# Five ScalarE weight casts of the third head pair get order edges in a decoder-trunk kernel

## The chip, the core and the metric

The kernel runs on one core of one Trainium2 chip. A core has TensorE (PE; matrix products, with weight loads shown as PEld), VectorE (DVE), ScalarE (ACT), GpSimd (POOL) and SyncE (SP, which issues most of the loads). The engines run side by side, each through its own list of instructions in order, and wait for one another at semaphores. The metric is the device time of one execution in microseconds (us), as a median over several runs; less is better.

## What is computed

The reference is a decoder trunk of two layers on 256 tokens of width 1024, in float32. Layer 0 mixes tokens with three dilated window attentions, layer 1 with a gated linear attention, and each is followed by a gated feed-forward block with a short convolution. What matters here is layer 0's token mixer:

```python
def dilated_mixture(h, w_in, w_out, rel_bias):
    B, S, _ = h.shape
    qkv = (h @ w_in).reshape(B, S, A_GROUPS, 3, A_HEADS, A_HEAD_DIM)
    scale = A_HEAD_DIM ** -0.5
    outs, lses = [], []
    for g, (window, dilation) in enumerate(A_CONFIGS):
        o, lse = dilated_branch(qkv[:, :, g, 0] * scale, qkv[:, :, g, 1], qkv[:, :, g, 2],
                                rel_bias[:, g * A_HEADS:(g + 1) * A_HEADS], window, dilation)
        ...
    wts = jax.nn.softmax(jnp.stack(lses), axis=0)
    o = jnp.sum(wts[..., None] * jnp.stack(outs), axis=0)
    return o.reshape(B, S, A_WIDTH).astype(h.dtype) @ w_out
```

There are three groups (dilations 1, 4, 16) and 16 heads of width 64, taken as eight pairs. Each pair needs queries, keys and values of all three groups.

## The kernel before

**Numbers in two parts.** Each float32 weight is split in a high part, a cast to TensorE's fp32r format, and a low part, the difference. `split` (L165) does that for one block: SyncE loads `raw` (L169), ScalarE casts it to `whi` in two pieces (L176), and VectorE subtracts to get `wlo` in two pieces (L182). The activations `h` have the same two parts, and each product is three products on TensorE (`mm3`, L200 to L205): high by high, and high by low both ways. `raw` rotates over four buffers, `whi` and `wlo` over three each.

**The pairs.** The loop at L666 runs over the pairs `u` = 0 to 7. Pairs 0 and 1 are projected together from one big block `w0` (L686 to L698). From the third pair (`u` = 2) on, a pair has three projections `g` = 0, 1, 2 (L705 on), each a block of 2048 columns (pieces of 1024) that gives the queries and keys of one group, and then its values in two halves (L751 on), each a block of 1536 columns (pieces of 768). TensorE goes through the eight row tiles `kt` of a projection in order; the first half of the values serves `kt` 0 to 3, the second 4 to 7, and each piece two of them.

**Evacuation.** `evacuate` (L610) takes a projection out of PSUM. For `g` = 0, ScalarE scales the queries (L621) and casts the keys (L622, the high part), VectorE makes the low parts (L625, L627), and GpSimd copies the keys to where the scores read them (L630). For the other groups ScalarE scales the queries and VectorE copies the keys (both L615). The list `evacuated` holds the last two instructions of this, ScalarE's first.

**Softmax and turning.** `scores` (L484) makes a pair's scores on TensorE (L496 to L510); VectorE adds the bias and takes the maximum (L529), and negates it (L547); ScalarE takes the exponentials (L550, recorded in the list `exps`, four for each pair); VectorE normalises (L539 to L543). `turn_all` (L570) transposes the probabilities on TensorE (L578) and copies them out of PSUM (L582, on ScalarE and VectorE). `outputs` (L584) multiplies with the values. The scores of the first pair run behind the values of the second pair. The scores of the second pair and both turns run between the projections of the third pair, so this pair's round holds more work than the later ones.

**Filling work.** The modulation terms of later blocks are dot products of weight rows with the condition, on VectorE (L142), each followed by a small ScalarE instruction (L150 or L152). `next_half` (L465) places them between the rest.

**The order of work.** The build orders each engine's instructions by a simulated timeline, with the order of the source as priority among what is ready. `behind(...)` (L275) adds edges by hand: each instruction that is made inside it and runs on the engine of a named instruction is ordered behind that one. An edge to a ScalarE instruction holds ScalarE's instructions alone, and it adds order, no semaphore. `split` takes such edges for its two casts in `after`, and for its subtractions in `low` and `late`. In the third pair, projection 2 has edges for its subtractions only (L706). Half 0 of the values has none for its casts, and its subtractions stand behind the last dot product so far. Of half 1 the first cast stands behind the scaled query copy of projection 2 (`second`, L745), and its subtractions behind the key copy; the second cast has no edge.

Of the kernel before, what the change touches and what calls it, by code (L numbers as in the profile page):

```python
# [59 lines left out]
def trunk(ctx: ExitStack, tc: tile.TileContext, I, out):  # L60
# [104 lines left out]
    def split(src, n, dmas=1, after=((), ()), late=(), low=(), lows=True, view=None):  # L165
        raw = wraw.tile([P, 2048], F32, tag="raw", name="raw")
        for i in range(dmas):
            c = slice(n * i // dmas, n * (i + 1) // dmas)
            last_load[0] = nc.sync.dma_start(raw[:, c], src[:, c])  # L169
        hi = wspl.tile([P, 2048], F32R, tag="whi", name="whi")  # L170
        lo = wspl.tile([P, 2048], F32R, tag="wlo", name="wlo")
        part = view or (lambda w: w)
        for i in range(0, n, n // 2):
            c = slice(i, i + n // 2)
            with behind(*after[i > 0]):
                copied[0] = nc.scalar.copy(part(hi[:, c]), part(raw[:, c]))  # L176
        if not lows:
            return hi, lo, raw, n // 2
        for i in range(0, n, n // 2):
            c = slice(i, i + n // 2)  # L180
            with behind(*(late if i else low)):
                last_lo[0] = nc.vector.tensor_tensor(part(lo[:, c]), part(raw[:, c]), part(hi[:, c].bitcast(F32)), op=ALU.subtract)  # L182
        return hi, lo
# [482 lines left out]
    for u in range(NPAIR):  # L666
        if u == 0:
            with tc.issue_after(last_load[0].ins):
                bias = load_bias(0)
        place = u % 2 if u < 4 else 1  # L670
        if u == 0:
            k_hi, k_lo = ([att.tile([P, T + 4 * (i or j)], F32R, tag=f"k0{i}{j}", name="k", bufs=1) for j in range(2)] for i in range(2))
            for z in k_lo:
                nc.gpsimd.memset(z[:, T:].bitcast(F32), 0.0)
        q, k = [q_pair[place][0]], [(q_pair[place][1], k_lo[place], k_hi[place])]
        for g in (1, 2):
            q.append(att.tile([P, T], F32, tag=f"q{g}", name="q"))
            k.append(att.tile([P, T], F32, tag=f"k{g}", name="k"))
        v = [att.tile([P, NG * P], F32, tag=f"v{t}", name="v") for t in range(2)]
        if u == 0:  # L680
            b0 = [bank("pqk", tg) for tg in "ssspp"]
            pqk = [b[:, T * i : T * i + T] for b in b0[:3] for i in range(2)]
            pv = b0[3:]
            b1 = [bank("pqk", "t") for _ in range(3)]
            pqk1 = [b[:, T * i : T * i + T] for b in b1 for i in range(2)]
            for kt in range(KT):  # L686
                s, e = kt == 0, kt == KT - 1

                for a, b in ((0, 0), (1, 0), (0, 1)):
                    for i in range(2 * NG):  # L690
                        w = parts(w0[kt], P * i)
                        mm(pqk[i], w[a], h[kt][b], start=s and i % 2 == 0 and (a, b) == (0, 0), stop=e and i % 2 == 1 and b == 1)  # L692
                wv = parts(w0[kt], 6 * P, NG * P)
                for a, b in ((0, 0), (1, 0), (0, 1)):
                    for t in range(2):
                        mm(pv[t][:, : NG * P], h[kt][a][:, P * t : P * t + P], wv[b], start=s and (a, b) == (0, 0), stop=e and b == 1)
                for i in range(2 * NG):
                    mm3(pqk1[i], parts(w0[kt], 9 * P + P * i), h[kt], s and i % 2 == 0, e and i % 2 == 1)  # L698
        if u == 0:
            first_values = [by_group(v[n], pv[n], n, True) for n in range(2)]  # L700
        if u < 2:
            for g in range(NG):
                evacuate(q, k, g, (pqk, pqk1)[u][2 * g], (pqk, pqk1)[u][2 * g + 1], *first_values[1:])
        else:
            for g in range(NG):  # L705
                low = negated[-1:] if (u, g) == (2, 2) else ()  # L706
                w = split(I["wqk"][u - 2, g], 2048, low=low, late=low)
                if (u, g) == (2, 2):
                    with behind(last_lo[0]):
                        for _ in range(4):  # L710
                            second_pair[2]()
                    for _ in range(2):
                        next_half(norms[-1], turned[1])
                if (u, g) == (2, 1):
                    with tc.issue_after(last_load[0].ins):
                        bias = load_bias(1)
                    with behind(last_lo[0]):
                        for _ in range(4):
                            before[2]()
                    with behind(done):  # L720
                        second_pair = scores(1, *held, bias, *mm_k)
                pqk = bank("pqk", "p")
                pq, pk = pqk[:, :T], pqk[:, T:]
                for kt in range(KT):
                    s, e = kt == 0, kt == KT - 1


                    hk = level if (u, g) > (3, 1) and g != 1 and kt == 0 else h[kt]
                    with behind(*(last_t if (g, kt) == (2, 0) else last_s if u == 2 and kt == 0 else [])):
                        mm3(pq[:, :T], parts(w, 2 * P * kt), hk, s, False)  # L730
                    mm_k = [mm3(pk[:, :T], parts(w, 2 * P * kt + P), hk, False, e)]
                if g == 1:
                    turn_all(before, pt := new_pt(), *mm_k)
                if (u, g) == (NPAIR - 1, 2):
                    copy_level((o_hi[OLEVEL], o_lo[OLEVEL]), *turned[-2:-1])
                done = evacuate(q, k, g, pq, pk)
                if (u, g) == (2, 2):
                    turn_all(second_pair, second_pt := new_pt(), *mm_k)
                if (u, g) == (2, 0):
                    first_loads.append(last_load[0])  # L740
                if u > 2:
                    for _ in range((3, 0, 3)[g]):
                        next_half(done)
                if g == 2 - (u > 2):
                    second = list(evacuated)  # L745
            if u == 4:
                with behind(last_load[0]):
                    nc.sync.dma_start(x_all, I["xT"])
        if u > 0:
            pv = [bank("pv", "p") for _ in range(2)]  # L750
            for half in range(2):  # L751
                with behind(*chain[7]):


                    if half == 1 and u < 4:
                        hi, lo = (first_values[:1], ()) if u == 1 else (second[:1], second[1:])
                    elif u == 2:
                        hi, lo = (), last_dot[:1]
                    else:
                        hi = lo = ()  # L760
                    w = split(I["wv"][u - 1, half], 1536, after=(hi, hi if u == 1 else ()), low=lo, late=lo if u == 2 else ())
                    if u == 2 and half == 1:
                        for _ in range(4):
                            next_half(last_lo[0])
                if u > 1 and half == 0:
                    with tc.issue_after(last_load[0].ins):
                        bias = load_bias(u)
                for k4 in range(4):
                    kt = 4 * half + k4
                    wv = parts(w, 384 * k4, 384)  # L770
                    for t in range(2):
                        ht = [y[:, P * t : P * t + P] for y in h[kt]]
                        with behind(*(last_t if u == 2 and kt == 0 else [])):
                            last_pv[:] = [mm3(pv[t][:, :384], ht, wv, kt == 0, kt == KT - 1)]
        for n in range(2 if u else 0):
            by_group(v[n], pv[n], n)
        if u == 0:
            first_pair = q, k, v, bias
            continue
        if u == 1:  # L780
            held = q, k, v
            before = scores(0, *first_pair, *last_pv)
            continue
        now = scores(u, q, k, v, bias, *last_pv)
        outputs(0 if u == 2 else u - 1, before, pt, last_s[0])
        if u == 2:
            outputs(1, second_pair, second_pt, last_po[0])
            copy_level(h[0], last_cast[0])
        before = now
# [386 lines left out]
    with behind(*chain[3]):  # L1176
        w = columns(0, 1)
# [309 lines left out]
```

## Time and profile before

| | us |
|---|---|
| runs: median of 3 (lowest to highest) | 761.14 (760.03 to 762.98) |
| profiled execution, own time | 759.74 |
| its span in the trace | 758.0 |

The span goes from the first to the last instruction of the trace; the profiled execution took 1.74 us more than that. The mean granted clock of TensorE in it was 0.999 of full speed.

How to read the rows that follow. On the page, busy time and its share of the span stand for each engine, and then the chain of work that ended last, followed back from the end, by engine. A row of the windows gives a stretch, its length, then busy time and number of instructions for each engine, the clock, the busy share of the DMA engines and what they moved in GB/s. A row of waits says who waited for whom: us in total, times, longest. A row of the timeline gives the start, the time that the row takes, engine, line, operation, the tiles (out<-in), shape and number of instructions merged; in brackets stands how long the engine had been idle before and what ended that. Products on TensorE overlap, so their pace is read from the distances of their starts, not from the time of one.

### The profile page before, as it was taken

Reading aid. Unit: us, or ns where it says so; the run is one execution under the profiler, and the core shown is the slowest. Engines: PE = TensorE matmul, PEld = TensorE weight load, DVE = VectorE, ACT = ScalarE, POOL = GpSimd, SP = SyncE. Lnnn points to the kernel's source line nnn. Section 1 sums busy time; section 2 is a strip of 40 time slices with the busy share of each in tenths; the row PEclk is TensorE's granted clock in tenths of the full one; section 3 lists DMA queues with packets and bytes.
Section 4 is the critical chain, followed back from the end, with each engine's and each line's share of the span. In section 5 each row is a group of like instructions: output and inputs, shape, how many; then the busy total and the mean of one; then the engine's idle time right before and its main releaser. Section 6 shows DMA issues by size and latency. Waiting matters only on the chain.

```text
span 758.0 us, 16066 instructions
## 1 busy us (share of the span) xinstructions
PE 750.3 (99%) x6416; PEld 733.0 (97%) x6416; DVE 649.5 (86%) x1190; ACT 483.0 (64%) x945; POOL 32.7 (4%) x57
## 2 busy tenths in 40 slices
PE   8999999999999999999999999999999999999997
PEld 5999999999999999999999999999999999999996
DVE  6988999988989779999999778977869999988592
ACT  6458666565656478676767556835967767676551
POOL 0002001101101010000000000000010000000100
PEclk9999999999999999999999999999999999999999
DMA  9989599888887358877646986864646767667621
GB/s 346 403 298 328 207 338 372 269 278 296 289 285 261 112 181 294 308 271 251 220 140 234 353 295 218 327 241 163 227 168 231 276 233 268 125 146 266 204 102 56
DMA packets 39481, 187.20 MB, mean 247 GB/s; under 512 B 9020, under 2 KB 11708, under 8 KB 25838
## 3 DMA queue, kind: packets, MB, share of 16 engines
q1 hardware_dynamic: 39024, 185.73, 70.3%
q8 instruction: 50, 0.82, 0.4%
q10 hardware_dynamic: 382, 0.45, 0.2%
q14 instruction: 25, 0.20, 0.1%
HBM read 185.06 MB, written 1.10 MB: 246 GB/s over the span
## 4 chain that ended last, share of the span: by engine, by line
PE 99%; DVE 0%; ACT 0%; DMA 0%; issue 0%; DVEq 0%; ACTq 0%
PE pab L204 10%; PE pab L203 10%; PE pab L205 10%; PE pqk L203 6%; PE pqk L205 6%; PE pqk L204 6%; PE pd L204 5%; PE pd L203 5%; PE pd L205 5%; PE pv L204 4%; PE pv L203 4%; PE pv L205 4%; PE pqk L692 2%; PE py L203 2%; PE py L205 2%; PE py L204 2%
## 5 line engine op out<-in xcount | busy, mean ns | idle before, releaser
L176 ACT CAST whi<-raw 128x1024 fp32r<-128x1024 f32 (+4 forms) x264 | 237.8, 946 | 97.1 <-PE pab L204 43.4
L182 DVE TENSOR_TENSOR wlo<-raw,whi 128x1024 fp32r<-128x1024 f32 (+5 forms) x248 | 263.7, 1092 | 30.0 <-ACT whi L176 29.4
L205 PE MATMUL pab<-hhi,wlo 128*128 128x256 f32 x680 | 187.0, 276 | 0.0
L204 PE MATMUL pab<-hlo,whi 128*128 128x256 f32 x680 | 186.9, 276 | 0.0
L203 PE MATMUL pab<-hhi,whi 128*128 128x256 f32 x680 | 185.1, 277 | 0.0
L204 PEld LDWEIGHTS pab<-hlo,whi 128*128 128x128 f32 x680 | 127.5, 188 | 0.2
L205 PEld LDWEIGHTS pab<-hhi,wlo 128*128 128x128 f32 x680 | 127.7, 188 | 0.0
L203 PEld LDWEIGHTS pab<-hhi,whi 128*128 128x128 f32 x680 | 126.5, 188 | 0.1
L142 DVE CUSTOM_DVE_ANT_0 ada_raw<-ada_raw,c_bc 128x1024 f32<-128x1024 f32 x96 | 114.5, 1229 | 5.6 <-DMA ada_raw<-in_w_ada 5.6
L203 PE MATMUL pqk<-hhi,whi 128*128 128x256 f32 x374 | 102.6, 279 | 0.0
L204 PE MATMUL pqk<-hlo,whi 128*128 128x256 f32 x374 | 102.0, 278 | 0.0
L205 PE MATMUL pqk<-hhi,wlo 128*128 128x256 f32 x374 | 101.5, 278 | 0.0
L204 PE MATMUL pd<-glo,whi 128*128 128x256 f32 x308 | 84.9, 276 | 0.0
L205 PE MATMUL pd<-ghi,wlo 128*128 128x256 f32 x308 | 84.9, 276 | 0.0
L203 PE MATMUL pd<-ghi,whi 128*128 128x256 f32 x308 | 84.7, 276 | 0.0
L203 PEld LDWEIGHTS pqk<-hhi,whi 128*128 128x128 f32 x374 | 69.9, 188 | 0.2
L204 PEld LDWEIGHTS pqk<-hlo,whi 128*128 128x128 f32 x374 | 69.9, 188 | 0.0
L205 PEld LDWEIGHTS pqk<-hhi,wlo 128*128 128x128 f32 x374 | 69.2, 188 | 0.7 <-issue 0.7
L204 PEld LDWEIGHTS pd<-glo,whi 128*128 128x128 f32 x308 | 57.8, 188 | 0.0
L205 PEld LDWEIGHTS pd<-ghi,wlo 128*128 128x128 f32 x308 | 57.8, 188 | 0.0
L203 PEld LDWEIGHTS pd<-ghi,whi 128*128 128x128 f32 x308 | 57.7, 188 | 0.0
L1003 ACT ACTIVATE r<-pab,small 128x256 f32<-128x256 f32 x86 | 47.2, 559 | 10.0 <-DVE r L1006 9.6
(277 smaller groups left out, 1461.1 us busy)
## 6 DMA issues: line engine op xcount, KB each, us to landing
raw<-in_w_up SPq DMA_DIRECT2D x42, 1024.0 KB, 4.9
ada_raw<-in_w_ada SPq DMA_DIRECT2D x29, 1024.0 KB, 6.0
raw<-in_w_down SPq DMA_DIRECT2D x28, 704.0 KB, 5.4
ada_raw<-in_w_ada SPq DMA_DIRECT2D x38, 512.0 KB, 6.8
raw<-in_wqk SPq DMA_DIRECT2D x18, 1024.0 KB, 5.7
raw<-in_wv SPq DMA_DIRECT2D x14, 768.0 KB, 6.7
raw<-in_w SPq DMA_DIRECT2D x7, 960.0 KB, 6.5
raw<-in_w_v_b SPq DMA_DIRECT2D x6, 768.0 KB, 6.1
```

The lines of the kernel that those rows point to most:

```text
L142: i = nc.vector.tensor_tensor_reduce(w, w, c_bc, op0=ALU.mult, op1=ALU.add, scale=1.0, scalar=0.0, accum_out=dot,)
L176: copied[0] = nc.scalar.copy(part(hi[:, c]), part(raw[:, c]))
L182: last_lo[0] = nc.vector.tensor_tensor(part(lo[:, c]), part(raw[:, c]), part(hi[:, c].bitcast(F32)), op=ALU.subtract)
L203: mm(ps, a[0], b[0], start=start, stop=False)
L204: mm(ps, a[0], b[1], start=False, stop=False)
L205: return mm(ps, a[1], b[0], start=False, stop=stop)
L692: mm(pqk[i], w[a], h[kt][b], start=s and i % 2 == 0 and (a, b) == (0, 0), stop=e and i % 2 == 1 and b == 1)
L1003: nc.scalar.activation(r, u[:, :T], AF.Identity, scale=cw[2], bias=col(C_CB + 44 * l + f))
```

## The change

Three edits. The list `ready` takes the ScalarE instruction of the third pair's first evacuation (the cast of the keys, L622), and both casts of projection 2's weights are ordered behind it. Both casts of half 0 of the third pair's values are ordered behind the eighth exponential (`exps[7]`, the last one of the second pair). The second cast of half 1 gets the edge that the first one has, behind the scaled copy of projection 2's queries. Nothing changes for other pairs, as the second pair's two casts had their edges before, and from the fourth pair on the second piece has none.

```diff
-                w = split(I["wqk"][u - 2, g], 2048, low=low, late=low)
+                w = split(I["wqk"][u - 2, g], 2048, after=(ready, ready) if (u, g) == (2, 2) else ((), ()), low=low, late=low)
...
+                if g == 0:
+                    ready = evacuated[:1]
...
                     if half == 1 and u < 4:
                         hi, lo = (first_values[:1], ()) if u == 1 else (second[:1], second[1:])
                     elif u == 2:
-                        hi, lo = (), last_dot[:1]
+                        hi, lo = exps[7:8], last_dot[:1]
                     else:
                         hi = lo = ()
-                    w = split(I["wv"][u - 1, half], 1536, after=(hi, hi if u == 1 else ()), low=lo, late=lo if u == 2 else ())
+                    w = split(I["wv"][u - 1, half], 1536, after=(hi, hi if u < 3 else ()), low=lo, late=lo if u == 2 else ())
```

## The prediction, made before the changed kernel was run

> **What bounds the kernel now.** I read the page first (busy time, then the chain that ended last), then the windows by stage around the moved casts, then who TensorE's weight load waited for, and last the timelines of ScalarE, VectorE and TensorE from 69 to 116 us.
>
> ```profile
> span 758.0 us, 16066 instructions
> PE 750.3 (99%) x6416; PEld 733.0 (97%) x6416; DVE 649.5 (86%) x1190; ACT 483.0 (64%) x945; POOL 32.7 (4%) x57
> PE 99%; DVE 0%; ACT 0%; DMA 0%; issue 0%; DVEq 0%; ACTq 0%
> ```
>
> The chain is TensorE for 99% of the span, and all other engines share the rest. ScalarE, the only engine that the change touches, is busy for 64%. So moving ScalarE's work pays only where TensorE waits for it, and costs only where TensorE is made to wait.
>
> ```profile
> core 0: us, PE busy (x) PEld busy (x) DVE busy (x) ACT busy (x) POOL busy (x), PEclk, DMA share, GB/s
> 75.50:84.40 8.90, 8.90 (x105) 8.56 (x103) 7.51 (x23) 5.32 (x15) 1.59 (x4) 1.00 0.49 189
> 84.40:91.10 6.70, 6.70 (x62) 6.70 (x60) 6.52 (x18) 3.58 (x10) 0.00 (x0) 1.00 0.55 140
> 91.10:99.80 8.70, 8.70 (x52) 8.44 (x51) 8.70 (x14) 5.80 (x10) 0.00 (x0) 1.00 1.00 393
> ```
>
> These are the stages of projections 1 and 2 and of the values of the third pair. TensorE counts as busy all the time in each, at full clock (1.00), and VectorE is full too in the third. Busy time hides short stalls because the ends are modelled, so I look at one wait and at the starts of the products around it.
>
> ```profile
> PEld pv L204 <- DVE wlo L182: 0.3, 1, 0.3
> 91.15 0.42 PE L203 MATMUL pv<-whi,hhi 128*128 128x384 f32 x1
> 95.39 0.34 PE L205 MATMUL pv<-whi,hlo 128*128 128x384 f32 x1
> 95.56 0.34 PE L203 MATMUL pv<-whi,hhi 128*128 128x384 f32 x1
> 95.85 0.45 PE L204 MATMUL pv<-wlo,hhi 128*128 128x384 f32 x1
> 96.13 0.34 PE L205 MATMUL pv<-whi,hlo 128*128 128x384 f32 x1
> ```
>
> Products of this size start 0.17 us apart (95.39 to 95.56). The two next steps take 0.29 and 0.28: 0.12 and 0.11 us too much. This stall of 0.23 us, at the first use of the second half of the third pair's value weights, is all that the touched stages can give back by having weights earlier.
>
> **The change part by part.** Five casts move on ScalarE: two of 1024 columns (projection 2), two of 768 (values, half 0), and the second of 768 of half 1; the first one of half 1 had its edge already. Nothing is added or taken away, no cast issues a transfer, and the buffers of the loads come free behind VectorE's subtraction (L182), which comes after the cast in any case.
>
> ```profile
> 69.50 2.00 ACT L176 CAST whi<-raw 128x1024 fp32r<-128x1024 f32 x2 [0.17 <-DMA raw<-in_wqk]
> 73.28 0.62 ACT L550 ACTIVATE prob<-prob,m 128x384 f32<-128x384 f32 x1 [1.22 <-DVE m L547]
> 75.89 1.57 ACT L176 CAST whi<-raw 128x768 fp32r<-128x768 f32 x2
> 77.49 0.77 ACT L621 ACTIVATE q<-pqk 64x256 fp32r<-64x256 f32 x2
> 78.28 0.37 ACT L622 CAST k<-pqk 128x256 fp32r<-128x256 f32 x1
> 82.07 0.62 ACT L550 ACTIVATE prob<-prob,m 128x384 f32<-128x384 f32 x1 [3.41 <-DVE m L547]
> 84.39 0.19 ACT L550 ACTIVATION_READ_ACCUMULATOR prob<-prob,m 128x1 f32 x1
> 84.48 0.82 ACT L176 CAST whi<-raw 128x768 fp32r<-128x768 f32 x1
> 90.15 0.37 ACT L615 ACTIVATE q<-pqk 128x256 f32<-128x256 f32 x1
> 90.41 2.72 ACT L176 CAST whi<-raw 128x768 fp32r<-128x768 f32 x3
> 78.69 0.86 DVE L625 SCALAR_TENSOR_TENSOR q<-pqk,q 64x256 fp32r<-64x256 f32 x2 [1.33 <-ACT k L622]
> 82.00 2.35 DVE L182 TENSOR_TENSOR wlo<-raw,whi 128x1024 fp32r<-128x1024 f32 x2
> ```
>
> *Projection 2's casts, 2.00 us at 69.50, go behind L622.* Their old place empties, but the first pair's exponentials at 73.28 had waited 1.22 us for VectorE after a gap, so they come no earlier: 0. The new place is the hole of 3.41 us between L622 and the second pair's exponentials, which 2.00 fits with 1.41 to spare. They then end near 78.65 + 2.00 = 80.65. Their cover is that TensorE first wants these weights at 84.38 (row below), and VectorE's subtraction of them stands at 82.00. So 0; if the hole were closed the casts would come behind the exponentials, which is the second rival.
>
> *The values' half 0, 1.57 us at 75.89, goes behind the second pair's last exponential.* It stood ahead of L621 without a pause, so L621 and L622 come up to 1.6 us earlier, and GpSimd's copies of the keys behind L622 with them. VectorE waited 1.33 us for L622 ahead of L625; with that gone, the second pair's scores on VectorE, the exponentials (80.74 for 82.07) and their successors come about 1.3 us earlier. None of it ends in a wait of TensorE: 0. The casts then run from 84.57 at the latest to 86.14. Their users:
>
> ```profile
> 90.16 1.82 DVE L182 TENSOR_TENSOR wlo<-raw,whi 128x768 fp32r<-128x768 f32 x2
> 91.89 0.42 DVE L615 COPY k<-pqk 128x256 f32<-128x256 f32 x1
> 92.23 0.95 DVE L182 TENSOR_TENSOR wlo<-raw,whi 128x768 fp32r<-128x768 f32 x1
> 93.10 1.22 DVE L142 CUSTOM_DVE_ANT_0 ada_raw<-ada_raw,c_bc 128x1024 f32<-128x1024 f32 x1
> 94.24 0.69 DVE L582 COPY pt<-t 128x512 f32<-128x512 f32 x1
> 94.84 0.95 DVE L182 TENSOR_TENSOR wlo<-raw,whi 128x768 fp32r<-128x768 f32 x1
> ```
>
> VectorE subtracts half 0 at 90.16 and TensorE starts on it at 91.15, so 4.0 us are left: 0. Queued behind these two casts are the scaled copy of projection 1's queries (L615) and two copies of transposes (L582), which would come up to 1.6 us later, or not later at all where the exponentials come earlier.
>
> *The values' half 1.* The second cast (84.48) goes behind the queries' copy at 90.15, as the first already does, inside the run of three at 90.41 (2.72 us is more than 3 x 0.82, so the other two of that run are wider ones, the next pair's). This is where the order of use matters. VectorE's subtraction at 92.23 can only be the second piece's, as that was cast at 84.48, while the first piece's stands at 94.84, ends at 95.79, and TensorE goes on at 95.85: the first piece, wanted first, is subtracted last, behind a dot product (1.22) and a copy (0.69). With both casts behind the query copy, the first ends at about 91.2 and the second at about 92.0. If VectorE's places stay and the first piece takes the one at 92.23, it is done at 93.2, over 2 us ahead of its use, and the second piece, at 94.84, is done at 95.8. That one is wanted 12 products after 95.56 (two matrices of 128 rows by two row halves by three), 12 x 0.173 = 2.1 us later. The stall goes: -0.23.
>
> No row shows the changed order of VectorE, so I bound it: -0.23 from above, as nothing else is waiting; +1.2 from below, where one more dot product (1.22) gets ahead of the first piece. I take -0.2, as the nearest rows are those of the present places, and keep both ends.
>
> Sum: 0 + 0 + 0 - 0.2. The profiled execution took 759.74 us, 1.74 around its span of 758.0, and gets 759.5. The median of the runs is 761.14, 1.40 above that execution, so the forecast is 760.9.
>
> **The rivals.**
>
> *The change doesn't do what it says.* The edges hold ScalarE only. VectorE may still subtract the second piece first, as its order is its own. TensorE then waits as before: 761.1. For it: in the rows above the first piece was cast by 91.2 and still stood behind three other instructions. Against it: the reason for the second piece's early place, an early cast, is gone.
>
> *Projection 2's casts fall behind the second pair's exponentials.* Against it is the hole of 3.41 us, in which nothing else is ready; for it, that the exponentials stand earlier in the source. The first cast would then run 84.57 to 85.5, its subtraction (half of 2.35) would end at 86.7, and TensorE, which wants it two products after its start, would stand from about 84.6:
>
> ```profile
> 83.15 1.47 PE L578 MATMUL t<-ident,pn 128*128 128x128 f32 x12
> 84.38 0.37 PE L203 MATMUL pqk<-hhi,whi 128*128 128x256 f32 x1
> 89.92 1.47 PE L578 MATMUL t<-ident,pn 128*128 128x128 f32 x12
> 77.39 0.39 PE L203 MATMUL pqk<-hhi,whi 128*128 128x256 f32 x1
> ```
>
> That costs 2.1 us: 763.2. Only with the two value casts ahead as well (1.57), and the query copy and a transpose copy behind them (about 1), does it reach 4.7 us and 765.8. From 3.8 us it decides the sign beyond 0.5%. The Trainium skill (TensorE: Matmul & The Clock Gate, HAM oscillation) says that TensorE idle for over some 3.4 us falls back to half clock; by that, the longer form would cost an estimated 1.7 us more, and the shorter nothing. The granted clock is 1.00 in every window above, so the rows here can't show it.
>
> *Later rounds are ordered worse (slower).* The build orders each engine by a simulated timeline, so new ends of ScalarE's work at 75 to 92 us may change which of VectorE's ready instructions goes first later on. Room in a later round:
>
> ```profile
> 104.20:133.50 29.30, 29.30 (x272) 28.55 (x268) 26.79 (x55) 19.34 (x45) 3.08 (x4) 1.00 0.93 341
> 113.09 0.28 DVE L543 TENSOR_SCALAR pn<-prob,m 128x128 f32<-128x128 f32 x1
> 115.23 1.47 PE L578 MATMUL t<-ident,pn 128*128 128x128 f32 x12
> ```
>
> VectorE is busy 26.8 of 29.3 us, and the probabilities are ready 1.9 us (113.37 to 115.23) ahead of their transposes. It decides once more than 1.9 us, two dot products of 1.22, goes ahead of them: then each round loses at least 0.5, and a third dot product makes it 1.8. Five rounds of about 1.2 cost 6 us: 767. Against it: TensorE paces each stage, and the moved work is all within the third pair's.
>
> *Faster than forecast.* Projection 1's 48 products take 5.76 us (77.39 to 83.15), projection 2's 48 take 5.54 (84.38 to 89.92), 4.6 ns less for each. If projections 0 and 1 got the later pace, 0.44 would be gained: 760.5. Nothing in the change reaches TensorE's pace.
>
> **How the numbers follow.** I call 0.5% (3.8 us) what a measurement of this kernel can tell from no change. The forecast gets 0.60, the first rival 0.12, the second 0.12 (0.07 in its short form, 0.05 in the long one), the third 0.12, the fourth 0.04, half of which I give to a median that falls low beyond 0.5%. Within 0.5%: 0.60 + 0.12 + 0.07 + 0.02 = 0.81. Slower: 0.05 + 0.12 = 0.17. Faster: 0.02. The range, 758.9 to 764.9 us, holds the forecast, the first rival, the short form of the second and part of the fourth, with the runs before themselves spread from 760.03 to 762.98.
>
> **What would show it.** Right: no cast of 1024 columns between 69 and 73 us on ScalarE; two between L622 and the second pair's exponentials, which start near 80.7; VectorE's wait of 1.33 ahead of L625 gone; two casts of 768 behind the exponentials; TensorE's wait for wlo at L204 gone, and product starts near 95.6 evenly 0.17 apart. Wrong: TensorE waiting for whi or wlo at 84 to 92 us (second rival), or transposes at L578 waiting for pn in the rounds after 104 us (third), or the wait of 0.3 still there (first).

## The result, and the profile after

The changed kernel takes 758.42 us (median of 22 runs, 757.16 to 764.16); the kernel before, beside it, 761.05 (22 runs, 758.55 to 765.88). The ratio is 0.9971, 95% interval 0.9959 to 0.9983. At 761 us that is 2.2 us less (1.3 to 3.1): small, inside the bound of 0.5%, but not nothing, and eleven times the 0.2 us that was forecast. The measured time lies 0.5 us below the range.

The profiled executions, taken alone, say the opposite. The one of the changed kernel took 760.39 us. From its page, the span, the busy time and the chain by engine:

```profile
span 758.6 us, 16069 instructions
...
PE 749.2 (99%) x6416; PEld 733.1 (97%) x6416; DVE 649.8 (86%) x1190; ACT 482.5 (64%) x945; POOL 30.7 (4%) x57
...
PE 92%; DVE 4%; DMA 2%; ACT 1%; issue 0%; DVEq 0%; ACTq 0%
```

A span of 758.6 where before had 758.0, and a chain with only 92% TensorE where before had 99%. So one pair of profiles shows a slightly longer time and more waiting for other engines, and 22 runs show 2.6 us less between the medians. Which of the two profiles misleads, and where, is what the rest is about.

What ScalarE did, from its timeline in the changed kernel:

```profile
70.43 0.61 ACT L550 ACTIVATE prob<-prob,m 128x384 f32<-128x384 f32 x1 [1.53 <-DVE m L547]
...
73.18 0.78 ACT L621 ACTIVATE q<-pqk 64x256 fp32r<-64x256 f32 x2 [0.24 <-PE pqk L205]
73.99 0.38 ACT L622 CAST k<-pqk 128x256 fp32r<-128x256 f32 x1
74.26 2.00 ACT L176 CAST whi<-raw 128x1024 fp32r<-128x1024 f32 x2
77.91 0.62 ACT L550 ACTIVATE prob<-prob,m 128x384 f32<-128x384 f32 x1 [1.66 <-DVE m L547]
...
80.33 1.56 ACT L176 CAST whi<-raw 128x768 fp32r<-128x768 f32 x2
...
87.27 0.38 ACT L615 ACTIVATE q<-pqk 128x256 f32<-128x256 f32 x1 [0.56 <-PE pqk L205]
87.55 3.46 ACT L176 CAST whi<-raw 128x768 fp32r<-128x768 f32 x4
```

The order is the one that was worked out: the two casts of projection 2 stand behind L622, half 0's two behind the second pair's exponentials, half 1's two behind the scaled queries. But everything is earlier by more than was worked out: L621 starts at 73.18 for 77.49, and even the first pair's exponentials, ahead of all moved work, start at 70.43 for 73.28. TensorE's list of waits between 57 and 110 us, then the place of its one entry in the timelines of TensorE, VectorE and ScalarE:

```profile
PE pqk L203 <- ACT v L643: 0.9, 1, 0.9
```

```profile
102.13 0.39 PE L203 MATMUL pqk<-hhi,whi 128*128 128x256 f32 x1 [0.90 <-ACT v L643]
```

```profile
99.34 1.23 DVE L142 CUSTOM_DVE_ANT_0 ada_raw<-ada_raw,c_bc 128x1024 f32<-128x1024 f32 x1 [0.56 <-DMA ada_raw<-in_w_ada]
```

```profile
100.60 0.29 ACT L152 ACTIVATE mod<-dot,small 128x1 f32<-128x1 f32 x1 [1.66 <-DVE dot L142]
100.81 0.35 ACT L639 COPY v<-pv 64x256 f32<-64x256 f32 x1
...
101.81 0.26 ACT L643 COPY v<-pv 64x128 f32<-64x128 f32 x1
```

The wait for `wlo` at L204 is gone. A new one stands at the first product of the fourth pair's projection 0: it needs the PSUM bank that ScalarE's copies of the values (L639 to L643) free, and these are queued behind a small modulation instruction (L152) that itself waits 1.66 us for a dot product, and this one for its load.

**Why the profile of before misleads.** Until about 19 us TensorE ran at half pace in it. The same twelve warm-up products and the window from 12 to 15 us, first in the profile of before, then in the changed kernel's (columns of the windows as above):

```profile
14.02 2.93 PE L301 MATMUL warm<-ones_d 128*128 128x128 f32 x12
```

```profile
12.00:15.00 3.00, 3.00 (x10) 1.57 (x9) 2.52 (x3) 2.53 (x6) 0.00 (x0) 1.00 1.01 419
```

```profile
13.15 1.60 PE L301 MATMUL warm<-ones_d 128*128 128x128 f32 x12
```

```profile
12.00:15.00 3.00, 3.00 (x22) 2.23 (x21) 2.32 (x4) 3.00 (x8) 0.00 (x0) 1.00 1.02 422
```

The twelve products take 2.93 us for 1.60, and in the same 3 us 10 products run for 22 (not all of one kind). The column of the granted clock says 1.00 in both, but it counts time for which the trace holds no clock record as full. The first record, one of full clock, begins at 18.93 us in the profile of before, at 11.39 in the changed kernel's and between 8.96 and 12.35 in the eleven other profiles below. So neither this column nor the mean clock of 0.999 given for that profile holds the slow start. By the second pair's values TensorE is 2.85 us behind:

```profile
59.99 0.39 PE L203 MATMUL pv<-whi,hhi 128*128 128x384 f32 x1
```

```profile
57.14 0.39 PE L203 MATMUL pv<-whi,hhi 128*128 128x384 f32 x1
```

In no other profile of this study did the half pace last so long. The loads are not late with it (a row below shows one that lands at nearly the same time either way), so in this execution every load, cast and subtraction had about 3 us more room than in the two other profiles of this kernel, where TensorE reaches the same product at 57.34 and 56.63. The Trainium skill (TensorE: Matmul & The Clock Gate, Seeing it yourself) warns that trn2's trace events of the clock gate have been seen to be unreliable. This trace doesn't bear that out: its first record, at 18.93, falls where the pace of the products changes.

### The profile page after: what moved, and what is told of

Same layout as the page of the kernel before. It is cut to its first block, busy times and chain, and to the rows that moved or that the text cites. A ratio compares the mean times of both kernels' runs of the same rounds, so it can differ in the third digit from the quotient of the medians.

```text
span 758.6 us, 16069 instructions
## 1 busy us (share of the span) xinstructions
PE 749.2 (99%) x6416; PEld 733.1 (97%) x6416; DVE 649.8 (86%) x1190; ACT 482.5 (64%) x945; POOL 30.7 (4%) x57
## 4 chain that ended last, share of the span: by engine, by line
PE 92%; DVE 4%; DMA 2%; ACT 1%; issue 0%; DVEq 0%; ACTq 0%
PE pab L203 10%; PE pab L204 10%; PE pab L205 10%; PE pqk L203 6%; PE pqk L205 6%; PE pqk L204 6%; PE pd L204 4%; PE pd L203 4%; PE pd L205 4%; PE pv L205 3%; PE pv L203 3%; PE pv L204 3%; PE pqk L692 2%; PE py L203 2%; PE py L205 2%; PE py L204 2%
## 5 line engine op out<-in xcount | busy, mean ns | idle before, releaser
L204 PE MATMUL pab<-hlo,whi 128*128 128x256 f32 x680 | 187.8, 278 | 0.0
L204 PEld LDWEIGHTS pab<-hlo,whi 128*128 128x128 f32 x680 | 127.5, 188 | 0.2
L204 PE MATMUL pqk<-hlo,whi 128*128 128x256 f32 x374 | 102.0, 278 | 0.0
L204 PE MATMUL pd<-glo,whi 128*128 128x256 f32 x308 | 84.9, 276 | 0.0
L204 PEld LDWEIGHTS pqk<-hlo,whi 128*128 128x128 f32 x374 | 69.9, 188 | 0.0
L204 PEld LDWEIGHTS pd<-glo,whi 128*128 128x128 f32 x308 | 57.8, 188 | 0.0
```

What stands on the lines that cost most here:

```text
L204: mm(ps, a[0], b[1], start=False, stop=False)
```

## The experiments

To compare kernels whose profiles start differently I use one interval: from the second pair's first product of values (59.99 and 57.14 in the rows above) to the first product of the fourth pair's projection 0 (104.23 and 102.13). It holds the whole third pair, and TensorE's work in it is the same in all kernels. The smallest value seen is 44.03 us, with no wait on TensorE's list; what is over that is loss. Every interval is of one profiled execution; every ratio is against runs of the kernel before on the same chip (12 runs for a row, but 22 for the change and 6 for without_half1).

| kernel | edits | interval, us | over 44.03 | ratio [95%] |
|---|---|---|---|---|
| before, profile of the prediction | none | 44.24 | 0.21 | |
| before_again | none | 46.68 | 2.65 | 0.9999 [0.9987, 1.0012] |
| before_third | none | 47.62 | 3.59 | 1.0007 [0.9995, 1.0019] |
| only_half1 | 3 | 48.21 | 4.18 | 1.0013 [1.0001, 1.0025] |
| only_half0 | 2 | 46.31 | 2.28 | 1.0000 [0.9979, 1.0022] |
| without_proj2 | 2, 3 | 45.93 | 1.90 | 0.9993 [0.9977, 1.0010] |
| only_proj2 | 1 | 45.64 | 1.61 | 0.9974 [0.9961, 0.9988] |
| without_half1 | 1, 2 | 45.24 | 1.21 | 0.9970 [0.9958, 0.9982] |
| the change | 1, 2, 3 | 44.99 | 0.96 | 0.9971 [0.9959, 0.9983] |
| after_again | 1, 2, 3 | 44.34 | 0.31 | 0.9977 [0.9964, 0.9991] |
| all_mod_later | 1, 2, 3 and L152 moved | 44.03 | 0.00 | 0.9959 [0.9943, 0.9975] |
| before_pe_later | none, ten warm-up products more | 44.58 | 0.55 | 1.0012 [0.9997, 1.0028] |
| all_mod_pe_later | as all_mod_later, and the ten products | 44.03 | 0.00 | 0.9987 [0.9974, 1.0000] |

**The kernel before, a second and a third time.** Nothing edited.

> The kernel before, unchanged, for another profile and for the spread. Three theories. Hidden wait: in the profile of before TensorE's first products ran slowly until 18.7 us, which made it some 2.9 us late and hid that VectorE, ScalarE and the loads set the start of the fourth pair (ScalarE's value copies end at 104.14, TensorE goes on at 104.23). In an execution with fast products from 14 us on, TensorE then waits 2 to 3 us for L643 ahead of that start. Pace: before loses its time in the second feed-forward block, where a row of products can start 118 ns apart instead of 113; then such a profile has no wait over 0.5 us and about 2.7 us of slower products after 570 us. Chance: ratio to before 1.000 +-0.002 in any case; the spread of this run says how much a ratio of 0.997 is worth.

> The kernel before, unchanged, for a third profile. Theory: its clock comes early (first products at full pace by 15 us), a cast of projection 2 waits over 2 us for its load with the first pair's exponentials behind it, and TensorE's waits between 78 and 105 us sum to over 1.5 us. If the clock comes late (after 18 us) they are under 0.5 us. Ratio 1.000 +-0.0015.

Both ratios are 1 within their intervals. The profile of before_again has the early start (57.34 us at the second pair's values), but the wait for L643 that I had expected in it isn't there; the time goes elsewhere. ScalarE in it:

```profile
69.92 2.00 ACT L176 CAST whi<-raw 128x1024 fp32r<-128x1024 f32 x2 [2.84 <-DMA raw<-in_wqk]
71.95 0.26 ACT L642 COPY v<-pv 64x128 f32<-64x128 f32 x1
72.22 0.26 ACT L643 COPY v<-pv 64x128 f32<-64x128 f32 x1
72.38 0.62 ACT L550 ACTIVATE prob<-prob,m 128x384 f32<-128x384 f32 x1
...
75.68 1.57 ACT L176 CAST whi<-raw 128x768 fp32r<-128x768 f32 x2 [0.79 <-DMA raw<-in_wv]
77.28 0.77 ACT L621 ACTIVATE q<-pqk 64x256 fp32r<-64x256 f32 x2
...
81.86 0.62 ACT L550 ACTIVATE prob<-prob,m 128x384 f32<-128x384 f32 x1 [3.41 <-DVE m L547]
```

The load of projection 2's weights lands at the same time as in the prediction's profile (the cast starts at 69.92 for 69.50), but ScalarE is ready 2.84 us ahead of it, where it had waited 0.17. Two value copies and the first pair's exponentials stand behind that cast; VectorE's last work for the exponentials (L547, below) was done by 70.71, 1.67 us before they start. Then half 0's casts wait 0.79 for their load, and L621 stands behind these. VectorE in the same profile, its row in a later stage, and the same two VectorE instructions in the changed kernel:

```profile
70.42 0.29 DVE L547 TENSOR_SCALAR m<-m 128x2 f32<-128x2 f32 x2
73.72 0.17 DVE L539 RECIPROCAL m<-m 128x2 f32<-128x2 f32 x1 [3.01 <-ACT prob L550]
...
78.48 0.86 DVE L625 SCALAR_TENSOR_TENSOR q<-pqk,q 64x256 fp32r<-64x256 f32 x2 [2.03 <-ACT k L622]
```

```profile
90.00:99.00 9.00, 8.41 (x45) 7.84 (x46) 9.00 (x15) 6.39 (x11) 0.00 (x0) 1.00 1.01 347
```

```profile
71.77 0.17 DVE L539 RECIPROCAL m<-m 128x2 f32<-128x2 f32 x1 [1.25 <-ACT prob L550]
...
74.53 0.86 DVE L625 SCALAR_TENSOR_TENSOR q<-pqk,q 64x256 fp32r<-64x256 f32 x2
```

VectorE stands idle for 5.0 us (3.01 + 2.03), for 1.25 in the changed kernel, and is then busy 9.00 of 9.00 us. What it could have done in the hole it does late, and TensorE pays in small pieces. TensorE's waits from 57 to 110 us:

```profile
PE pqk L205 <- DVE wlo L182: 0.4, 1, 0.4
PE pv L204 <- DVE wlo L182: 0.4, 1, 0.4
PE pv L203 <- DVE k L615: 0.2, 1, 0.2
PE t L578 <- DVE m L529: 0.2, 1, 0.2
```

These show 1.2 us; the starts of the products, which the modelled ends don't touch, show 2.65. The loss in before_third is 3.59, and there the cast waits 2.72 us for the same load.

The time at which the fourth pair starts says the same, and doesn't hang on when TensorE reached the second pair's values: 104.23, 104.02 and 104.25 us in the three profiles of before, 102.13 and 101.02 in the two of the change. In the first of the three TensorE's late start happened to cost as much as the waits cost in the others.

**Edit 3 alone** (half 1's second cast). I first suspected the order of the loads: in the changed kernel SyncE issues the value weights ahead of rows for the dot products.

```diff
-                    w = split(I["wv"][u - 1, half], 1536, after=(hi, hi if u == 1 else ()), low=lo, late=lo if u == 2 else ())
+                    w = split(I["wv"][u - 1, half], 1536, after=(hi, hi if u < 3 else ()), low=lo, late=lo if u == 2 else ())
```

> Only the third edit: the second cast of half 1 of the third pair's values behind the queries' copy. It alone changes the order of SyncE's loads (both value halves go ahead of a weight row for a dot product) and VectorE's order after 90 us. Hidden wait, with the loads as its cause: ratio 0.997, as the whole change. The prediction's reading (only the 0.2 us wait for wlo goes): 0.9997. Pace: anything between 0.996 and 1.001, and the profile shows it after 570 us alone.

The ratio is 1.0013 (at least 1.0001): no gain, and the theory of the loads falls, as this edit alone brings the new order of loads. Its profile has the longest wait at the fourth pair, with ScalarE's timeline below it, and the window from 107 us after that:

```profile
105.39 0.39 PE L203 MATMUL pqk<-hhi,whi 128*128 128x256 f32 x1 [2.13 <-ACT v L643]
```

```profile
104.50 0.29 ACT L152 ACTIVATE mod<-dot,small 128x1 f32<-128x1 f32 x1 [2.01 <-DVE dot L142]
104.81 0.26 ACT L642 COPY v<-pv 64x128 f32<-64x128 f32 x1
```

```profile
107.00:110.00 3.00, 3.00 (x16) 3.00 (x15) 2.96 (x10) 0.53 (x3) 0.00 (x0) 0.50 0.76 276
```

**Edits 1 and 2, and edits 2 and 3.** The third edit, or the first, is taken back.

> The first two edits without the third: projection 2's casts behind the key cast, half 0's behind the exponentials. The loads stay in an order near that of before. Hidden wait, with the loads as its cause: ratio 1.000; with the early exponentials as its cause (SyncE waits 11.1 us for VectorE's scores before it can load the next bias): 0.997. Pace: no forecast, the profile shows it after 570 us.

> The last two edits without the first: projection 2's casts stay at their early place. VectorE's, TensorE's and SyncE's orders are those of the whole change, only ScalarE's differs. Hidden wait: ratio 0.997, as all that comes after the exponentials is the same. The wait at the start of the fourth pair stays under 1.2 us.

Without edit 3 the whole gain is there (0.9970, of six runs); a wait of 0.9 for `wlo` at L204 stays, which is as long as the one at L643 that the whole change has in its place. Without edit 1 hardly any gain can be seen (0.9993, interval over 1), where I had expected 0.997; the cast of projection 2 still waits 3.00 us for its load, and the fourth pair 1.53 us for L643, for the 1.2 at most that I had named. The gain hangs on edit 1.

**Edit 1 alone, edit 2 alone.**

```diff
-                w = split(I["wqk"][u - 2, g], 2048, low=low, late=low)
+                w = split(I["wqk"][u - 2, g], 2048, after=(ready, ready) if (u, g) == (2, 2) else ((), ()), low=low, late=low)
...
-                done = evacuate(q, k, g, pq, pk)
+                done = evacuate(q, k, g, pq, pk); ready = evacuated[:1] if g == 0 else ready
```

```diff
-                        hi, lo = (), last_dot[:1]
+                        hi, lo = exps[7:8], last_dot[:1]
...
-                    w = split(I["wv"][u - 1, half], 1536, after=(hi, hi if u == 1 else ()), low=lo, late=lo if u == 2 else ())
+                    w = split(I["wv"][u - 1, half], 1536, after=(hi, hi if u == 1 or (u, half) == (2, 0) else ()), low=lo, late=lo if u == 2 else ())
```

> The first edit alone: projection 2's casts behind the key cast. Theory from the second profile of before: ScalarE's list holds casts that wait for their loads (2.84 us at 69.92, 0.79 us at 75.68) ahead of work that TensorE soon needs, and TensorE, once its clock comes early, then waits 2.4 us in all between 81 and 96 us. With this edit the first pair's exponentials come some 2 us earlier, but half 0's casts still stand ahead of the query scaling (L621) and wait for their load, so L621 starts near 77 us as before and the gain is small: ratio 0.9995 to 1.0005, TensorE's waits from 81 to 96 us still about 2 us. Rival, that the late exponentials of the first pair are what counts: 0.997.

> The second edit alone: half 0's casts behind the second pair's exponentials. Same theory: L621 no longer stands behind casts that wait for a load, so it starts near 75 us for 77.3, the second pair's scores come 2 us earlier, and TensorE's waits from 81 to 96 us shrink from 2.4 to under 1 us: ratio 0.9975 to 0.9985. Rival, that the first edit carries the gain: 1.000.

Both went against what I had expected. ScalarE in only_proj2, then in only_half0:

```profile
73.25 0.78 ACT L621 ACTIVATE q<-pqk 64x256 fp32r<-64x256 f32 x2 [0.25 <-PE pqk L205]
74.06 0.37 ACT L622 CAST k<-pqk 128x256 fp32r<-128x256 f32 x1
74.33 3.46 ACT L176 CAST whi<-raw 128x1024 fp32r<-128x1024 f32 x4
```

```profile
69.47 2.00 ACT L176 CAST whi<-raw 128x1024 fp32r<-128x1024 f32 x2 [2.83 <-DMA raw<-in_wqk]
...
74.46 0.77 ACT L621 ACTIVATE q<-pqk 64x256 fp32r<-64x256 f32 x2
```

Edit 1 alone gives 0.9974, as much as the whole change within the intervals, and it moves all four casts: the row of four (3.46 us, less than 4 x 1.0, so the last two are the narrower ones) holds half 0's as well, which the build placed behind projection 2's without an edge. Edit 2 alone moves half 0's only; L621 comes 2.8 us earlier than in before_again, but the wait of 2.83 us at the head of the list stays, and the ratio is 1.0000. So half 0's place alone brings no gain that the runs can tell (the interval begins at 0.9979), and the removal of projection 2's cast from the head of the list is needed for it. Whether edit 1 would still give all of it with half 0's casts held ahead of L621 was not tried.

**The whole change, with the new wait taken away.** The small ScalarE instruction of the last of the four dot products (L152) is ordered behind the first value copies and no longer stands ahead of them. The edit is against the changed kernel:

```diff
-                        for _ in range(4):
+                        for _ in range(3):
...
-            by_group(v[n], pv[n], n)
+            freed = by_group(v[n], pv[n], n) if n == 0 else (by_group(v[n], pv[n], n), freed)[1]
+        if u == 2:
+            next_half(last_lo[0], freed)
```

> The whole change, and the small ScalarE instruction behind the last dot product (L152) one place later in ScalarE's list, behind the first four value copies of the third pair. One place in one list is all that differs from the changed kernel. Theory: the value copies then no longer wait for a dot product of VectorE that waits for its load, and TensorE's wait of 0.9 us for L643 ahead of the fourth pair goes: ratio to before 0.9955 to 0.9965, 0.001 below the changed kernel's 0.9971. Rival, the copies were late for another reason: 0.997, with the wait still there.

It came as expected: 757.17 us, ratio 0.9959, the lowest time of all. ScalarE, and TensorE at the fourth pair:

```profile
99.84 0.37 ACT L639 COPY v<-pv 64x256 f32<-64x256 f32 x1 [0.77 <-PE po L595]
...
100.87 0.26 ACT L643 COPY v<-pv 64x128 f32<-64x128 f32 x1
101.35 0.29 ACT L152 ACTIVATE mod<-dot,small 128x1 f32<-128x1 f32 x1 [0.22 <-DVE dot L142]
```

```profile
101.29 0.39 PE L203 MATMUL pqk<-hhi,whi 128*128 128x256 f32 x1
```

The bracket behind TensorE's row is gone and the interval is 44.03. It beats the kernel before beyond doubt. Against the change (0.9971) the step of 0.0012, 0.9 us, fits the wait that was removed (0.9 in the change's first profile, 0.2 in its second, below), but the intervals overlap.

**The whole change, unedited, once more.**

> The changed kernel, unchanged, for a second profile. Theory: ratio 0.997 +-0.0015; TensorE's waits between 60 and 105 us sum to 0.7 to 1.2 us and stand at L203 ahead of the fourth pair, behind L643. The slower product pace in the second feed-forward block (118 ns for 113) may be there or not, in any of these kernels; if it is always there in this one and never in before, the change would be to blame for it.

The ratio is 0.9977, and the wait at L643 is 0.2 us this time, below the 0.7 that I had named as the least: it differs from one execution to the next. Its chain begins with a load, in the rows above.

The runs by themselves also speak against chance. The kernel before was run 138 times in all, and its fastest run took 758.44 us; 19 of the 34 runs of the change are faster than that. Another mix of the two product paces that the last section describes could not do this, as profiles of both kernels show both paces.

**TensorE made late on purpose.** If a late TensorE hides the waits, ten more warm-up products at the start should cost little in the kernel before, and their full time where nothing waits.

```diff
-        keep_warm(6)
+        keep_warm(16)
```

> The kernel before with ten more warm-up products, about 2.2 us of TensorE at full clock, ahead of the first projection; the other engines' lists are the same. Theory: TensorE isn't the bound up to 96 us in most executions, since it waits 2.4 us for ScalarE and VectorE there, so the added 2.2 us are nearly free: ratio 1.000 to 1.001, and the waits from 81 to 96 us fall below 0.5 us. Rival, the prediction's reading, TensorE bound all the way: 1.003.

> The kernel of all_mod_later with the same ten added warm-up products as before_pe_later. In all_mod_later TensorE had no wait left between 57 and 105 us, so here the added 2.2 us should show in full, up to what the loads of the first block hide of it: 0.002 to 0.003 above that kernel's 0.9959, that is 0.998 to 0.999, against 0.001 for the same products in the kernel before. Rival, TensorE isn't the bound here either: 0.996 to 0.997.

In the profile of before_pe_later TensorE reaches the second pair's values at 58.76, 1.42 later than in before_again, and the fourth pair at 103.34, 0.68 earlier; the loss shrinks from 2.65 to 0.55. In this execution a later TensorE hides the waits. But it is the fastest of the twelve runs (759.30 us); their median is 762.67, 0.0028 over the 760.57 of the kernel before beside them. By the ratios the ten products cost 0.0012 in the kernel before and 0.0028 (0.9987 less 0.9959) with all waits gone. The one profile of all_mod_pe_later has TensorE only 0.41 later than all_mod_later at the second pair's values (57.67 for 57.26); its clock records also begin 3.1 us earlier (9.15 for 12.25). So the runs don't show that the products cost less in the kernel before: intervals of 0.0013 to 0.0016 to each side hold both, and by the medians there is hardly a difference.

## Why the prediction was wrong

**The reading of the bound failed.** "This stall of 0.23 us, at the first use of the second half of the third pair's value weights, is all that the touched stages can give back by having weights earlier." In the execution that I read, that is right: its interval is 44.24, 0.21 over the best. But that execution had its TensorE 2.85 us late from the start, and the loss that the usual execution has there (2.65 and 3.59 in the two others) did not show. The forecast was taken from the median of the runs, 761.1, which by these two profiles has this loss, and from a sum made where it was hidden. Over the two other profiles of before the interval is 47.15 on average, over the two of the change 44.67: 2.5 us, inside the 1.3 to 3.1 of the runs. So the step that failed is the bound itself, the 0.23 us taken as all that there was to gain: the runs showed about 2.2 us, out of waits behind one blocked list on ScalarE.

**The price of the moved casts failed with it.** "Their old place empties, but the first pair's exponentials at 73.28 had waited 1.22 us for VectorE after a gap, so they come no earlier: 0", and "None of it ends in a wait of TensorE: 0". In the two other profiles of before the old place of projection 2's casts holds a wait of 2.84 and 2.72 us for their load, with the exponentials queued behind it. The quoted row carried the hint: `[0.17 <-DMA raw<-in_wqk]`. A wait of 0.17 us behind a load says that the load and ScalarE were neck and neck, so an execution in which ScalarE comes earlier turns it into a long one. I read it as no wait.

**Right, in the trace of after:** the order on ScalarE, L621 no longer behind half 0's casts, no wait ahead of L625, half 1's casts together behind the scaled queries, the wait for `wlo` at L204 gone. The exponentials, forecast 1.3 us earlier, came 3.95 earlier than in before_again, which starts alike (77.91 for 81.86): not the time of two casts but that of the whole blocked list.

**Missed: the next wait.** Nothing was priced at the fourth pair. Its projection waited for L643, 0.9 us in one profile and 0.2 in the other. In the profile of before these copies ended at 104.14 and TensorE started at 104.23: a margin of 0.09 us that I had not looked for.

**The edits' shares were the wrong way round.** I had given the whole gain to half 1 (-0.2). Edit 3 alone is at 1.0013, and the change without it at 0.9970.

**The rivals.** Projection 2's casts did not fall behind the exponentials, and TensorE did not wait for `pn` in the rounds after 104 us. The change did what it says. The pace of the products brought nothing to the third pair. No rival stood for a gain larger than the one stall and a few tenths of pace, so nothing held the range open on that side.

## What to carry to other kernels

A wait on a list of waits is a difference of two arrival times, and one profile has one draw of each: look for what is within some 3 us of biting, the shift between two executions here (a bracket of 0.17 behind a load, a copy that ends 0.09 ahead of its user), and profile the same kernel two or three times before calling a stage free of loss. On an engine that works in order, whatever waits for a load should not stand ahead of work whose inputs are there. And when such a block is gone, look at the next consumer: here one small instruction ahead of the value copies took part of the gain back, and moving it gave the lowest time, 0.9959.

## What the runs showed of the hardware that was not expected

**Half pace after a wait of 2.13 us.** In only_half1 the window from 107 to 110 us, quoted above, holds 16 products at a granted clock of 0.50; in the profile of the change it holds 29 at 1.00. TensorE's timeline shows where it begins:

```profile
106.53 0.30 PE L203 MATMUL pqk<-hhi,whi 128*128 128x256 f32 x1
106.64 0.40 PE L204 MATMUL pqk<-hlo,whi 128*128 128x256 f32 x1
106.84 0.41 PE L205 MATMUL pqk<-hhi,wlo 128*128 128x256 f32 x1
107.05 0.41 PE L203 MATMUL pqk<-hhi,whi 128*128 128x256 f32 x1
```

At 106.64, 1.25 us after TensorE's wait at L643 ended, the distance of the starts goes from 0.11 to 0.21 us, and the trace's clock records hold half clock from 106.65 to 110.06. The Trainium skill (TensorE: Matmul & The Clock Gate, What's actually happening) gives half clock after at least one idle window of some 3.4 us; here half clock followed a wait of 2.13, behind a stretch of small products. This is one execution, and that the wait was the cause was not tested. In the changed kernel, with its 0.9, all windows there read 1.00.

**Two paces at full clock.** In the second feed-forward block the products run at one of two spacings for the whole stretch from 575 to 636 us. The windows of the change's profile and of after_again's, the same kernel:

```profile
575.00:636.00 61.00, 61.00 (x520) 61.00 (x520) 57.56 (x98) 42.77 (x75) 0.00 (x0) 1.00 0.71 243
```

```profile
575.00:636.00 61.00, 61.00 (x539) 61.00 (x539) 59.26 (x101) 45.03 (x79) 0.00 (x0) 1.00 0.75 259
```

That is 520 products or 539 in 61 us, 117 or 113 ns each, at 1.00 in both; 19 products are 2.2 us. The slower one is in the profiles of the change, only_half0 and before_third, so it goes with the execution and not with an edit. It is the main reason why the profiled span of the change (758.6) is no shorter than that of before, though the change is 2.1 us ahead at the fourth pair (102.13 for 104.23), and why after_again's is 754.8. What sets it is open.
